# S5 output matrices on two engines, the Toeplitz expansion moved behind the context's steps, and modulation matrices stored by load, in a hybrid S5/RWKV-7 layer

## The chip, the core and the metric

The kernel runs on one core of a Trainium2 chip. The metric is the device time of one execution in microseconds; the time before is the median of three runs. TensorE (PE) multiplies matrices and has a granted clock of one of two levels, 1.2 and 2.4 GHz; the profile gives it as a share of the higher one. VectorE (DVE, V in the code), ScalarE (ACT, A_) and GpSimd (POOL, Pg) compute element by element. SyncE (SP) issues every DMA of this kernel, in order, and waits at the head of its queue for what the next DMA needs.

## The reference

The layer runs over 512 latent tokens x and 256 context tokens of width 1024, with one set of weights:

```python
x = half_ffn(x, mod_x, 0, ...)             # norm, modulate, SwiGLU of 2816, gated add
ctx = half_ffn(ctx, mod_c, 0, ...)
hc = modulate(ctx, norm_g[l, 1], mod_c[3], mod_c[4])
hx = modulate(x, norm_g[l, 1], mod_x[3], mod_x[4])
out_c, ctx_states = token_mixers(hc, 1, zero_states(ctx.shape[0]), p, need_ctx)
out_x, _ = token_mixers(hx, rows, ctx_states, p, True)
x = x + mod_x[5] * out_x
x = half_ffn(x, mod_x, 2, ...)
```

`mod_x` and `mod_c` are nine vectors of 1024, silu(c) @ w_mod + b_mod, so `w_mod` is a matrix of 1024 x 9216. `token_mixers` multiplies by `w_in` and runs two mixers: a bidirectional S5 scan (32 groups of 16 channels, 64 complex states) and a bidirectional RWKV-7 scan. The context gives only its final states. The S5 scan is linear:

```python
hr, hi = _cmul(ab_re, ab_im, h0_re, h0_im)
_, _, s_re, s_im = lax.associative_scan(_s5_combine, (a_re, a_im, xr, xi), axis=0)
y = jnp.einsum('lbgp,gip->blgi', s_re, c_re) - jnp.einsum('lbgp,gip->blgi', s_im, c_im)
```

## The kernel before, in words

Every large product runs on TensorE with the weights split in two parts: `w_loads` issues a DMA of 512 KB into a tile `raw`, `w_split` makes `wh` on ScalarE and `wl` = raw - wh on VectorE or GpSimd, and `mm3` does three matmuls for each block (wh by hi, wh by lo, wl by hi). The list of all weight items in their order is `self.items`; `dense` goes through it.

The order of instructions is fixed when the program is built. All work is written as generators ("streams"); each yields what it needs next: tiles, names of events (`sch.post` posts them), or pairs such as ("V", 600), which mean that the engine's queue may be at most 600 ns ahead of TensorE's. `Plan` keeps an estimate of the time at which each engine is free (`RATE`, `LAT`), treats GpSimd and VectorE's instructions with two SBUF inputs as users of one port (`shared`), costs a DMA by its bytes alone, and always resumes the ready stream with the lowest priority number. `dense` has priority 9, so it fills what the others leave. `w_split` takes VectorE when GpSimd's queue is too far ahead.

S5 runs in blocks of eight tokens. For that `s5_build` (priority S5P = 3) makes, from the powers `pw` of the discretised state matrix, 16 pairs of input matrices (`X`, transposed and stored in DRAM as `GTd`), 16 pairs of output matrices (`H`, stored as `Hd`), and the direct terms of a block (`Kd`). From `Kd` it lays out `KTd` with 15 DMAs of 32 KB and from that the Toeplitz matrices `KTe` with eight of 256 KB. Input matrices are made by GpSimd (six instructions of 128x256 each), output matrices by VectorE in a stream of its own, `outputs`, with two steps ("halves") for each matrix. `GTd` is used by `s5_in` of the context and of x, `Hd` and `KTe` only by `s5_out`, late in the program.

At the start `mods01` and `bg_a` compute modulations 0 to 4: `mod_run` loads tiles `wmod` of 512 KB with four buffers (40 loads) and multiplies each with `zs`; `fill_run` does modulations 5 to 8 later with two buffers (32 loads). The context's FFN and then x's FFN run in `dense`, with the context's `w_in` items mixed into x's FFN.

`ctx_run` holds the context's chain. After the context's norm it adds `s5_build` and the streams of RWKV's preparation (`conv`, `v_rows`, `pn`, `pa`, `pb`), then waits for event `s5b`, for the context's products and for four rounds of `pb` and `v_rows`; then it frees their memory and adds the steps: `rw_solve`, `rw_pre`, `rw_main`, `s5_in`, `s5_rec`. When they are done (events step3 and s5recc) it opens the pools of the next stage and posts `rwc` and `fp0x2`. The last four items of x's FFN (`tail`) wait for `fp0x2`, and the norm that follows waits for `rwc`. After it come x's own `w_in` items, its preparation and its steps (`phase_b2`), the merge and the second FFN (`phase_c`).

Of the kernel before, what the change touches and what calls it, by code (L numbers as in the profile page):

```python
# [11 lines left out]
OP = mybir.AluOpType  # L12
# [3 lines left out]
D, KT = 1024, 8  # L16
# [14 lines left out]
S5V = 600  # L31
S5Q = 3000
MPV = 1200
SPLIT_AT = 0
S5P = 3
# [248 lines left out]
class Kern:  # L284
# [9 lines left out]
    def bank(self, i):  # L294
        return self.psp.tile([128, 512], F32, name=f"b{i}")
# [232 lines left out]
    def mod_run(self, todo, pool, bufs, bank, loaded=None, step=None, done=None):  # L528


        nc, ws = self.nc, []
        steps = [(j, u, k) for j, u in todo for k in (0, 4)]

        def load(n):
            while len(ws) < min(n, len(steps)):
                j, u, k = steps[len(ws)]
                if loaded:
                    loaded(len(ws))
                ws.append(pool.tile([128, 4, 256], F32, name="wmod", bufs=bufs))
                nc.sync.dma_start(ws[-1], self.a["wmod"][j, :, k:k + 4, u * 256:(u + 1) * 256])  # L540
                if loaded and len(ws) == len(steps):
                    loaded(len(ws))

        for n, (j, u, k) in enumerate(steps):
            load(n + bufs)
            if step:
                step(n)
            if k == 0:
                pr = self.bank(bank(j))[:, 0:256]
            yield [ws[n], self.zs]  # L550
            for i in range(4):
                nc.tensor.matmul(pr[i * 32:i * 32 + 32], self.zs[:, k + i], ws[n][:, i], start=k == 0, stop=k == 4)
            if k == 0:
                continue
            row = pool.tile([128, 256], F32, name="mrow")
            nc.scalar.copy(row, pr)
            yield [row]
            pt = self.bank(6)
            for m in range(2):
                nc.tensor.matmul(pt[:, 2 * m:2 * m + 2], row[:, m * 128:(m + 1) * 128], self.sel, start=True, stop=True)  # L560
            ks = slice(2 * u, 2 * u + 2)
            nc.vector.tensor_add(self.mod[:, j, ks], pt[:, 0:4].rearrange("p (m v) -> p m v", v=2),
                                 self.bmod[:, j, ks, None].to_broadcast([128, 2, 2]))
            if done:
                done(j, u)
# [391 lines left out]
    def s5_build(self, sb):  # L957
        nc, a = self.nc, self.a
        V, A_, Pg, PE = nc.vector, nc.scalar, nc.gpsimd, nc.tensor
# [86 lines left out]
        half = lambda n: sb.tile([128, 2, 256], F32, name=n, bufs=1 + (n == "X"))  # L1046
# [6 lines left out]
        todo = [(d, h2) for d in range(2) for h2 in range(8)]  # L1053
# [5 lines left out]
        def load(n, name, src):  # L1059
            t = sb.tile([128, 2, 2, 16], F32, name=name, bufs=2)  # L1060
            d, h2 = todo[n]
            c = slice(d * 16 + h2 * 2, d * 16 + h2 * 2 + 2)
            for i in range(2):
                nc.sync.dma_start(t[:, i], src[i, :, c])
            return t, c

        def outputs():

            nxt = load(0, "hc", a["s5C"])
            for n, (d, h2) in enumerate(todo):  # L1070
                (Ct, c), nxt = nxt, load(n + 1, "hc", a["s5C"]) if n < 15 else None
                yield [Ct, ("V", S5V)]
                H, ms = half("H"), half("mh")
                ks = slice(1, 9) if d == 0 else slice(8, 0, -1)
                for o, (r0, b0, r1, b1, op) in enumerate(terms):
                    V.tensor_mul(r4(ms[:, 0]), bk(pw, r0, ks, c), bb(Ct[:, b0]))
                    V.tensor_mul(r4(ms[:, 1]), bk(pw, r1, ks, c), bb(Ct[:, b1]))
                    if o == 0:
                        V.tensor_tensor(H[:, 0], ms[:, 0], ms[:, 1], op=OP.subtract)
                    else:  # L1080
                        V.scalar_tensor_tensor(H[:, 1], ms[:, 0], -1.0, ms[:, 1], op0=OP.mult, op1=OP.subtract)
                    yield [("V", S5V)]
                for r in range(2):
                    nc.sync.dma_start(self.Hd[2 * h2:2 * h2 + 2, :, d, r].rearrange("e p f -> p e f"),
                                      H[:, r].rearrange("p (e f) -> p e f", e=2))
            self.sch.post("s5h")

        self.sch.add(outputs(), S5P)
        nb, nx = load(0, "hb", a["s5B"]), load(0, "hk", a["s5C"])
        for n, (d, h2) in enumerate(todo):  # L1090
            (B, c), (Ct, c) = nb, nx
# [4 lines left out]
            X, ms = half("X"), half("ms")  # L1096
# [19 lines left out]
            for e in range(2):  # L1116
                o = pk[:, e * 32:(e + 1) * 32]
# [2 lines left out]
            ks = sb.tile([128, 64], F32, name="kst")  # L1120
            A_.copy(ks, pk[:, 0:64])
            nc.sync.dma_start(Kd[d, :, h2 * 64:(h2 + 1) * 64], ks)
        yield ["s5h"]

        Kt, kz = [[half(n).rearrange("p a b -> p (a b)") for n in t] for t in (("X", "H"), ("ms", "mh"))]
        for d in range(2):
# [14 lines left out]
        for s in range(8):  # L1141
            src = [t[s * 16:(s + 1) * 16].rearrange("p (g o) -> p g o", o=16) for t in Kt]
            nc.sync.dma_start(self.KTd[:, :, 14 - s], src[0])
            if s:
                nc.sync.dma_start(self.KTd[:, :, 7 - s], src[1])
        yield [self.KTd]
        for s in range(8):
            nc.sync.dma_start(self.KTe[s], self.KTd[:, :, 7 - s:15 - s].rearrange("i g l o -> i g (l o)"))
        self.sch.post("s5b")


    def win_items(self, r):
# [940 lines left out]
def layout(i):  # L2093
    f = lambda t: np.ascontiguousarray(t)
    o = {}
    o["xin"] = f(i["x"][0].reshape(NX, KT, 128).transpose(2, 1, 0))
    o["cin"] = f(i["ctx"][0].reshape(NCT, KT, 128).transpose(2, 1, 0))
    o["cc"] = f(np.stack([i["c"][0].reshape(KT, 128).T, i["c_ctx"].reshape(KT, 128).T], axis=2))
    o["wmod"] = f(i["w_mod"][0].reshape(KT, 128, 9, 1024).transpose(2, 1, 0, 3))
    o["bmod"] = f(i["b_mod"][0].reshape(9, KT, 128).transpose(2, 0, 1))  # L2100
    o["ng"] = f(i["norm_g"][0].reshape(3, KT, 128).transpose(2, 0, 1))
    o["fg"] = f(i["final_g"].reshape(KT, 128).T)
    g = i["ffn_w_gate"][0].reshape(2, KT, 128, FT, 128).transpose(0, 3, 2, 1, 4)
    u = i["ffn_w_up"][0].reshape(2, KT, 128, FT, 128).transpose(0, 3, 2, 1, 4)
    o["wgu"] = f(np.stack([g, u], axis=2))
    o["wdn"] = f(i["ffn_w_down"][0].reshape(2, FT, 128, 4, 256).transpose(0, 3, 2, 1, 4)).reshape(2, 4, 128, FT, 2, 128)
    gi = np.arange(512).reshape(4, 8, 16).transpose(0, 2, 1).reshape(512)
    win = i["w_in"][0][:, np.concatenate([gi, np.arange(512, 4480)])]
    o["win"] = f(win.reshape(KT, 128, 35, 128).transpose(2, 1, 0, 3))
    o["cw"] = f(i["rwkv_conv"][0].reshape(9, 12, 128).transpose(2, 1, 0))  # L2110
    o["w2"] = f(i["rwkv_w2"][0].reshape(128, 512))
    o["a2"] = f(i["rwkv_a2"][0].reshape(128, 512))
    o["wv"] = f(np.stack([i["rwkv_w0"][0], i["rwkv_a0"][0]]).reshape(2, 2, 4, 128).transpose(3, 0, 1, 2))
    kv = [i["rwkv_k_k"][0], i["rwkv_k_a"][0], i["rwkv_r_k"][0].reshape(512), i["s5_D"][0]]
    o["kv"] = f(np.stack(kv).reshape(4, 4, 128).transpose(2, 0, 1))
    gq = lambda t: np.moveaxis(t.reshape((2, 16, 2) + t.shape[2:]), 2, 0)
    A = lambda t: f(np.moveaxis(gq(t[0]), 3, 1).reshape(128, 32))
    B = lambda t: f(np.moveaxis(gq(t[0]), 3, 1).reshape(128, 32, 16))
    C = lambda t: f(np.moveaxis(gq(t[0]), 4, 1).reshape(128, 32, 16))
    o["s5A"] = np.stack([A(i["s5_A_re"]), A(i["s5_A_im"])])  # L2120
    o["s5B"] = np.stack([B(i["s5_B_re"]), B(i["s5_B_im"])])
    o["s5C"] = np.stack([C(i["s5_C_re"]), C(i["s5_C_im"])])
    o["ldt"] = f(gq(i["s5_log_dt"][0]).reshape(2, 32))
    t4 = lambda w, n: f(w.reshape(4, 128, n, 2, 128).transpose(2, 1, 3, 0, 4)).reshape(n, 128, 8, 128)
    o["wglu"] = t4(i["s5_w_glu"][0][gi][:, gi], 2)
    o["wproj"] = t4(i["s5_w_proj"][0][gi], 4)
    o["wo"] = t4(i["rwkv_w_o"][0], 4)
    o["wout"] = f(i["w_out"][0].reshape(KT, 128, KT, 128).transpose(2, 1, 0, 3))
    o["g2"] = f(i["rwkv_g2"][0])
    o["ln"] = f(np.stack([i["rwkv_ln_g"][0], i["rwkv_ln_b"][0]]).reshape(2, 4, 128).transpose(2, 0, 1))  # L2130
    o["s5D"] = f(i["s5_D"][0].reshape(1, 512))
    return o
# [17 lines left out]
```

## Time and profile before

| what | value |
| --- | --- |
| median of three runs | 1881.02 us (1879.26 to 1885.11) |
| the profiled execution, its own time | 1882.93 us |
| its span, first to last instruction | 1881.2 us |
| TensorE busy | 1681.7 us, 89% |
| VectorE, ScalarE, GpSimd busy | 1008.5, 716.1, 655.1 us |
| mean granted clock of TensorE | 0.935 |
| DMA | 278.42 MB, mean 148 GB/s |

All times below are microseconds from the span's start in this one execution. "Busy" is the union of an engine's instructions; an instruction that is held up while it runs counts as busy. Nearly every row has line L209, that of the helper that records all instructions, so the rows are told apart by the names of their tiles: out<-in.

### The profile page before, as it was taken

Reading aid. Unit: us, or ns where it says so; the run is one execution under the profiler, and the core shown is the slowest. Engines: PE = TensorE matmul, PEld = TensorE weight load, DVE = VectorE, ACT = ScalarE, POOL = GpSimd, SP = SyncE. Lnnn points to the kernel's source line nnn. Section 1 sums busy time; section 2 is a strip of 40 time slices with the busy share of each in tenths; the row PEclk is TensorE's granted clock in tenths of the full one; section 3 lists DMA queues with packets and bytes.
Section 4 is the critical chain, followed back from the end, with each engine's and each line's share of the span. In section 5 each row is a group of like instructions: output and inputs, shape, how many; then the busy total and the mean of one; then the engine's idle time right before and its main releaser. Section 6 shows DMA issues by size and latency. Waiting matters only on the chain. (4 is left out here: it accounts for less than half of the span.)

```text
span 1881.2 us, 33153 instructions
## 1 busy us (share of the span) xinstructions
PE 1681.7 (89%) x13208; PEld 1409.2 (75%) x13208; DVE 1008.5 (54%) x1763; ACT 716.1 (38%) x1200; POOL 655.1 (35%) x799
## 2 busy tenths in 40 slices
PE   6899999899999989768976879969799999999996
PEld 3699997778887877666544657758689988888886
DVE  3376563755558737444788755644357533333335
ACT  3355442445453213434434323434443342222221
POOL 0134231466664313721334526950015321111111
PEclk9999989899999999887988969979899999999998
DMA  9956551335555464424753484637555223233331
GB/s 308 326 179 193 185 157 58 108 104 148 147 162 150 142 195 154 119 94 130 228 182 101 135 252 150 171 108 199 168 200 181 68 79 101 90 99 102 96 96 56
DMA packets 235626, 278.42 MB, mean 148 GB/s; under 512 B 93617, under 2 KB 186801, under 8 KB 234449
## 3 DMA queue, kind: packets, MB, share of 16 engines
q1 hardware_dynamic: 235472, 276.32, 48.3%
q8 instruction: 104, 1.70, 0.4%
q14 instruction: 50, 0.40, 0.1%
HBM read 234.31 MB, written 43.22 MB: 148 GB/s over the span
## 5 line engine op out<-in xcount | busy, mean ns | idle before, releaser
L209 PE MATMUL b<-hx,wh 128*128 128x512 f32 (+1 forms) x2432 | 704.6, 377 | 19.0 <-ACT wh L209 10.6
L209 POOL TENSOR_TENSOR wl<-raw,wh 128x1024 fp32r<-128x1024 f32 x119 | 292.2, 2457 | 805.7 <-ACT wh L209 748.4
L209 PEld LDWEIGHTS b<-hx,wh 128*128 128x128 f32 x2432 | 444.4, 197 | 103.7 <-issue 16.2
L209 PE MATMUL b<-hx,wl 128*128 128x512 f32 (+1 forms) x1216 | 451.4, 371 | 7.5 <-POOL wl L209 6.5
L209 DVE TENSOR_TENSOR wl<-raw,wh 128x1024 fp32r<-128x1024 f32 x154 | 213.2, 1385 | 291.0 <-ACT wh L209 288.7
L209 ACT CAST wh<-raw 128x1024 fp32r<-128x1024 f32 x273 | 283.1, 1046 | 192.8 <-DMA raw<-in_wgu 67.8
L209 PEld LDWEIGHTS b<-hx,wl 128*128 128x128 f32 x1216 | 238.2, 196 | 48.1 <-POOL wl L209 8.8
L209 PE MATMUL b<-ah,wh 128*128 128x512 f32 (+1 forms) x560 | 196.3, 351 | 0.0
L209 PE MATMUL b<-ah,wl 128*128 128x512 f32 (+1 forms) x560 | 194.4, 347 | 0.3 <-POOL wl L209 0.3
L209 PE MATMUL b<-al,wh 128*128 128x512 f32 (+1 forms) x560 | 194.6, 347 | 0.0
L209 PE MATMUL b<-hc,wh 128*128 128x256 f32 x928 | 174.1, 289 | 1.5 <-ACT hc L209 1.2
L209 PEld LDWEIGHTS b<-hc,wh 128*128 128x128 f32 x928 | 146.5, 193 | 12.6 <-issue 10.0
L209 PE MATMUL b<-hc,wl 128*128 128x256 f32 x464 | 132.0, 284 | 0.0
L209 PEld LDWEIGHTS b<-ah,wl 128*128 128x128 f32 x560 | 107.4, 192 | 13.5 <-POOL wl L209 0.5
L209 PEld LDWEIGHTS b<-ah,wh 128*128 128x128 f32 x560 | 107.3, 192 | 12.7 <-issue 0.2
L209 ACT CAST ah<-prod 128x512 fp32r<-128x512 f32 (+1 forms) x68 | 36.6, 538 | 210.6 <-DVE prod L209 210.6
L209 PEld LDWEIGHTS b<-al,wh 128*128 128x128 f32 x560 | 107.3, 192 | 12.5 <-DVE al L209 0.4
L209 ACT ACTIVATE sil<-b 128x512 f32<-128x512 f32 (+1 forms) x68 | 35.0, 515 | 153.6 <-PE b L209 153.5
L209 DVE TENSOR_TENSOR prod<-sil,b 128x512 f32<-128x512 f32 (+1 forms) x68 | 39.6, 582 | 95.2 <-PE b L209 75.7
L209 PEld LDWEIGHTS b<-hc,wl 128*128 128x128 f32 x464 | 89.6, 193 | 0.0
L209 DVE SCALAR_TENSOR_TENSOR x1c<-b,gp,x1c 128x512 f32<-128x512 f32 (+1 forms) x67 | 43.9, 662 | 74.5 <-PE b L209 74.5
L209 PE MATMUL b<-wmod,zs 128*32 128x256 f32 x576 | 55.7, 478 | 23.4 <-DMA wmod<-in_wmod 23.1
(289 smaller groups left out, 2327.4 us busy)
## 6 DMA issues: line engine op xcount, KB each, us to landing
raw<-in_wgu SPq DMA_DIRECT2D x132, 512.0 KB, 3.8
wmod<-in_wmod SPq DMA_DIRECT2D x72, 512.0 KB, 5.5
raw<-in_wdn SPq DMA_DIRECT2D x66, 512.0 KB, 3.7
raw<-in_win SPq DMA_DIRECT2D x49, 512.0 KB, 3.9
gt<-GTd SPq DMA_DIRECT2D x32, 256.0 KB, 4.0
abk<-st SPq DMA_DIRECT2D x8, 1024.0 KB, 5.8
AB<-abk SPq DMA_DIRECT2D x8, 1024.0 KB, 6.9
GTd<-gst SPq DMA_DIRECT2D x16, 256.0 KB, 2.4
```

What stands on the lines that cost most here:

```text
L209: r = f(out, *args, **kw)
```

## The change

Three edits. The array `wmod` is laid out on the host so that the 4 KB that a load brings to a partition are contiguous in DRAM; before they were four runs of 1 KB. The stream `outputs` exists twice: on VectorE from the first matrix on, and on GpSimd from the last one back, entered by `s5_build` itself when all input matrices are done; both take from one list, `left`. GpSimd's writes into the tiles of the input matrices (`hb`, `X`, `ms`). The scalar form of the second half is replaced by a sign flip of the small tile `Ct` and a plain subtraction. And the eight DMAs from `KTd` to `KTe` wait for event `rwc`, with `s5b` posted before them.

```diff
-                nc.sync.dma_start(ws[-1], self.a["wmod"][j, :, k:k + 4, u * 256:(u + 1) * 256])
+                nc.sync.dma_start(ws[-1], self.a["wmod"][j, u, k // 4])
...
-        def outputs():
-
-            nxt = load(0, "hc", a["s5C"])
-            for n, (d, h2) in enumerate(todo):
-                (Ct, c), nxt = nxt, load(n + 1, "hc", a["s5C"]) if n < 15 else None
-                yield [Ct, ("V", S5V)]
-                H, ms = half("H"), half("mh")
+        left = list(range(16))
+
+        def outputs(V, e, names, end):
+
+            nxt = None
+            while left or nxt:
+                nxt = nxt or [left.pop(end)]
+                if len(nxt) == 1:
+                    nxt += load(nxt[0], names[0], a["s5C"])
+                n, Ct, c = nxt
+                d, h2 = todo[n]
+                nxt = None
+                if left:
+                    n = left.pop(end)
+                    nxt = [n, *load(n, names[0], a["s5C"])]
+                yield [Ct, (e, S5V if e == "V" else S5Q)]
+                H, ms = half(names[1]), half(names[2])
                 ks = slice(1, 9) if d == 0 else slice(8, 0, -1)
                 for o, (r0, b0, r1, b1, op) in enumerate(terms):
+                    if o:
+                        V.tensor_scalar(Ct[:, 1], Ct[:, 1], -1.0, None, op0=OP.mult)
                     V.tensor_mul(r4(ms[:, 0]), bk(pw, r0, ks, c), bb(Ct[:, b0]))
                     V.tensor_mul(r4(ms[:, 1]), bk(pw, r1, ks, c), bb(Ct[:, b1]))
-                    if o == 0:
-                        V.tensor_tensor(H[:, 0], ms[:, 0], ms[:, 1], op=OP.subtract)
-                    else:
-                        V.scalar_tensor_tensor(H[:, 1], ms[:, 0], -1.0, ms[:, 1], op0=OP.mult, op1=OP.subtract)
-                    yield [("V", S5V)]
+                    V.tensor_sub(H[:, o], ms[:, 0], ms[:, 1])
+                    yield [(e, S5V if e == "V" else S5Q)]
...
-            self.sch.post("s5h")
+            self.sch.post("s5h" + e)
...
-        self.sch.add(outputs(), S5P)
+        self.sch.add(outputs(V, "V", ("hc", "H", "mh"), 0), S5P)
...
-        yield ["s5h"]
+        yield from outputs(Pg, "P", ("hb", "X", "ms"), -1)
+        yield ["s5hV"]
...
-        yield [self.KTd]
+        self.sch.post("s5b")
+        yield ["rwc", self.KTd]
         for s in range(8):
             nc.sync.dma_start(self.KTe[s], self.KTd[:, :, 7 - s:15 - s].rearrange("i g l o -> i g (l o)"))
-        self.sch.post("s5b")
...
-    o["wmod"] = f(i["w_mod"][0].reshape(KT, 128, 9, 1024).transpose(2, 1, 0, 3))
+    o["wmod"] = f(i["w_mod"][0].reshape(2, 4, 128, 9, 4, 256).transpose(3, 4, 0, 2, 1, 5))
```

S5V is 600 and S5Q is 3000.

## Rows read from the trace of the kernel before

**Rows 1.** The page's first part: busy time, share of the span, instructions.

```profile
PE 1681.7 (89%) x13208; PEld 1409.2 (75%) x13208; DVE 1008.5 (54%) x1763; ACT 716.1 (38%) x1200; POOL 655.1 (35%) x799
```

**Rows 2.** Busy time by stretches: stretch, length, engines, TensorE's clock, DMA share, GB/s.

```profile
core 0: us, PE busy (x) PEld busy (x) DVE busy (x) ACT busy (x) POOL busy (x), PEclk, DMA share, GB/s
0.00:50.00 50.00, 34.88 (x218) 19.30 (x222) 16.94 (x58) 15.94 (x34) 3.68 (x10) 1.00 0.94 310
50.00:100.00 50.00, 41.77 (x389) 30.68 (x381) 19.61 (x40) 17.53 (x34) 8.15 (x9) 0.97 0.95 314
150.00:200.00 50.00, 50.00 (x426) 49.96 (x425) 29.51 (x42) 23.98 (x35) 18.59 (x9) 1.00 0.62 198
...
17.00:21.00 4.00, 2.57 (x18) 0.73 (x18) 2.89 (x10) 2.58 (x7) 0.00 (x0) 1.00 1.10 348
75.00:79.00 4.00, 3.99 (x40) 2.95 (x39) 1.52 (x4) 1.13 (x3) 0.00 (x0) 1.00 1.04 398
```

**Rows 3.** TensorE's waits, 0 to 112 us: total, times, longest.

```profile
PE b L209 <- DMA wmod<-in_wmod: 14.2, 14, 5.0
```

**Rows 4.** Busy time by stretches around the context's chain, columns as in rows 2.

```profile
545.00:663.00 118.00, 115.99 (x654) 94.38 (x653) 86.67 (x145) 45.64 (x71) 47.85 (x34) 1.00 0.52 147
663.00:698.00 35.00, 34.13 (x150) 27.56 (x148) 12.16 (x14) 7.47 (x9) 8.57 (x13) 1.00 0.67 176
698.00:704.00 6.00, 0.61 (x10) 0.40 (x9) 0.00 (x0) 0.00 (x0) 0.00 (x0) 0.78 1.11 331
704.00:751.50 47.50, 45.96 (x394) 36.05 (x391) 36.17 (x66) 14.75 (x42) 15.73 (x15) 0.92 0.52 165
751.50:806.00 54.50, 37.95 (x802) 33.43 (x801) 20.73 (x43) 26.84 (x50) 38.88 (x119) 0.85 0.42 103
```

**Rows 5.** TensorE's timeline from 750 us: start, us, what, idle time before it.

```profile
750.92 0.39 PE L209 MATMUL b<-al,wh 128*128 128x512 f32 x1
751.15 0.39 PE L209 MATMUL b<-ah,wl 128*128 128x512 f32 x1
751.47 1.11 PE L209 MATMUL b<-AB 64*128 64x64 f32 x16
758.39 2.30 PE L209 MATMUL b<-AB 64*128 64x64 f32 x16 [5.82 <-DVE M L209]
```

**Rows 6.** SP's timeline from 662 us: start, us, DMA, count.

```profile
684.73 0.62 SPq L209 DMA_DIRECT2D KTd<-H  x1
...
686.45 6.35 SPq L209 DMA_DIRECT2D KTe<-KTd  x8
692.90 0.64 SPq L209 DMA_DIRECT2D AB<-abk  x1
...
695.98 0.78 SPq L209 DMA_DIRECT2D AT<-lf  x1
...
698.34 0.43 SPq L209 DMA_DIRECT2D gt<-GTd  x1
```

**Rows 7.** Tiles hc and H: ns min/median/max, first and last start, shapes.

```profile
L209 DVE TENSOR_TENSOR mh<-pw,hc x64: 400/419/2627, 349.5 to 661.8; 128x256 f32<-128x256 f32 x64
L209 DVE SCALAR_TENSOR_TENSOR H<-mh x13: 424/425/2508, 567.1 to 662.2; 128x256 f32<-128x256 f32 x13
L209 DVE TENSOR_TENSOR H<-mh x12: 424/426/1809, 582.8 to 661.0; 128x256 f32<-128x256 f32 x12
```

**Rows 8.** Tile st of the context's pb on GpSimd, columns as in rows 7.

```profile
L209 POOL TENSOR_TENSOR st<-kt,em x8: 677/686/1688, 416.8 to 590.0; 64x256 f32<-64x256 f32 x8
```

**Rows 9.** TensorE's waits, 900 to 1000 us.

```profile
PE b L209 <- DMA wmod<-in_wmod: 7.6, 6, 3.2
```

**Rows 10.** Tiles hb and X on GpSimd, columns as in rows 7.

```profile
L209 POOL TENSOR_TENSOR ms<-pz,hb x64: 636/650/1636, 349.2 to 542.6; 128x256 f32<-128x256 f32 x64
L209 POOL TENSOR_TENSOR X<-ms x32: 722/739/1599, 350.8 to 543.3; 128x256 f32<-128x256 f32 x32
```

**Rows 11.** Timeline of GpSimd and VectorE around 600 us.

```profile
599.90 2.57 POOL L209 TENSOR_TENSOR wl<-raw,wh 128x1024 fp32r<-128x1024 f32 x1 [9.15 <-ACT wh L209]
600.25 2.50 DVE L209 SCALAR_TENSOR_TENSOR H<-mh 128x256 f32<-128x256 f32 x1
```

**Rows 12.** GpSimd's timeline from 685 us.

```profile
687.44 0.91 POOL L209 TENSOR_SCALAR_AFFINE_SELECT mask<-ones 64x64 f32<-64x64 f32 x4 [10.18 <-DMA KTd<-H]
```

**Rows 13.** SP's timeline from 804 us.

```profile
806.61 3.69 SPq L209 DMA_DIRECT2D raw<-in_win  x2
830.58 7.57 SPq L209 DMA_DIRECT2D x1d<-x  x16
```

## The prediction

> **What bounds the kernel now.** I read the engine summary first. TensorE is busy 89% of the span and no other engine comes near [rows 1], so an edit counts only where TensorE waits, runs at its lower clock, or is kept waiting by a chain of other work. The busy time by stretches then says where that is, and two of those places touch the change.
>
> The first is the start. In the first two stretches of 50 us the DMA engines are busy 94 and 95% of the time, while TensorE is busy 34.9 and 41.8 us of 50, so it idles 23.4 us in all [rows 2]. The list of waits names the modulation matrices as the largest cause, 14.2 us in 14 waits [rows 3]. From 150 to 200 us TensorE has no gap [rows 2], so time won before that moves everything after it forward.
>
> The second is the end of the context's work. TensorE is full from 545 to 698 us, loses almost all of 698 to 704, is full again to 751.5, and then is busy 38.0 us of 54.5 at a mean granted clock of 0.85 [rows 4]. In the timeline of TensorE the last FFN matmul ends at about 751.5 and only the context's small matmuls follow, up to 806 [rows 5]: the tail of the FFN waits for the context's steps (event fp0x2), and TensorE has nothing else. Going back along the context: its loads (AB, Z, AT, U, gt) stand in SP's queue behind the eight KTe copies, which end at 692.8 [rows 6], and these stand behind the assembly that waits for VectorE's last output at 662.7 [rows 7]. The context's convolutions and its pb stage were done by 592: GpSimd's last st instruction starts at 590.0 [rows 8]. So from 592 to 692 the context waits for S5's output matrices and what follows them, and for nothing else.
>
> **The change part by part.**
>
> *Modulation matrices by load.* Each of the 72 loads keeps its 512 KB but moves runs of 4 KB where it moved runs of 1 KB. Where such loads alone are in flight (17 to 21 us) the DMA engines move 348 GB/s at full share; where nearly all that moves is weights and x in runs of 4 KB (75 to 79 us), 398 GB/s [rows 2]. The 40 loads of the start are 21.0 MB: 60.3 us at the one rate, 52.7 at the other, 7.6 us less, or 0.19 per load. The first 16 loads come before any other work: 3.0 us. The other 24 are worth 4.6 us, and overlap matmuls that fill TensorE for most of that time; I take half, 2.3. The sum is -5 us, bounded by -2 (SP's wait for a free buffer and the latency of a load stay) and -8. The 32 later loads fill gaps between other work; the waits on them from 900 to 1000 us are 7.6 us in 6 waits [rows 9]. 32 times 0.19 is 6 us of transfer, but those gaps follow VectorE's chain, so I take -1, bounds 0 and -3. The Trainium skill, "DMA: Bandwidth & Descriptors", section Specifications, puts the smallest transfer that reaches line rate at 512 bytes, by which 1 KB runs would gain nothing from the new layout; the two rates of this trace disagree. By that rule the sum below would lose both of these terms.
>
> *Output matrices by two engines.* One output is four multiplications and two subtractions. On VectorE they take a median of 0.42 us each, 2.5 us in all [rows 7]; the sign flip of a 32-column tile that replaces the scalar form adds under 0.2. On GpSimd the input matrices have the same six instructions: 4 x 0.65 + 2 x 0.74 = 4.1 us [rows 10]. Of VectorE's 32 halves 25 start after 566 us [rows 7], so 12.5 outputs are still to come when GpSimd finishes its inputs at about 545. Before, VectorE took 96 us for these, 7.7 each, since it also serves the FFN. GpSimd is busy 47.9 us of the 118 between 545 and 663 [rows 4], 41%; in the rest it could make an output every 4.1 / 0.59 = 6.9 us. Both together: 12.5 / (1/7.7 + 1/6.9) = 45 us, so the last output at 590 in place of 662.7. That is the early bound. The late bound is the two engines in each other's way. At 600.25 VectorE's subtraction takes 2.50 us while GpSimd's 2.57 us split runs beside it, six times its median [rows 11]. If the pair is always taken, an output on GpSimd costs 1.6 us more than on VectorE; six of them give 10 us more, and the last output falls at 673.
>
> GpSimd's outputs are also put ahead of what pb has for it: a stream of outputs may run up to 3000 ns ahead (S5Q) while pb asks for under 1000. Six outputs at 4.1 us delay the last pb from 592 to some 617, which alone would not hold the context.
>
> *KTe behind the steps.* The eight copies occupy SP for 6.35 us ahead of the context's loads [rows 6]. Without them the loads start at 686.5; GpSimd's mask, which waits for the last KTd copy until 687.4 [rows 12], limits this to about 5.5 us. At the new place, behind event rwc, the loads of the next weights queue behind them. When rwc falls after the FFN they cost nothing: SP issues only two loads from 806 to 830 [rows 13]. When it falls before, each weight load may be up to 6.35 us late; the loads run about two items of 24 matmuls ahead, so I take +1, bounds 0 and +3.
>
> *What an earlier start is worth.* Call t the time at which the context's loads start, 692.9 before [rows 6]. From there to 806 the chain takes 113 us. TensorE's own work from 692.9 to 806 is 5.1 + 0.6 + 46.0 + 38.0 = 89.7 us [rows 4], so with no gap it would end at 782.6, 23 us earlier; the stretches with clocks of 0.92 and 0.85 could give 3 more. The chain stays covered without any stretching if t is 669 or less. With FFN matmuls between its pieces it stretches: a step has about ten pieces, each may stand behind three matmuls that start 0.23 us apart [rows 5], four steps, so up to 28 us. For t I have 590 + 24 = 614 by the early bound (the 24 us from the last output to the start of KTe) and 697 by the late one. The row at 600 us is real but GpSimd idles more than half of that stretch, so I take the middle, 650. Then the chain ends at 650 + 113 + 28 = 791 with all of the stretching, after the 782.6 of TensorE's own work: 15 us less than 806. Bounds are -26 (no gap, full clock) and 0 (t = 693). Behind 806 the same streams follow in the same order, so I carry the gain to the end undiminished.
>
> **The sum.** -5 - 1 - 15 + 1 = -20 us. The profiled execution took 1882.9 us around its span of 1881.2, so it becomes 1863; it stood 1.9 us above the median of 1881.0, so for the median I say 1861. The best bounds together (-8 - 3 - 26) give 1844; the worst that still have an earlier t (-2 + 3 - 6) give 1876.
>
> **The rivals.** *Two engines in each other's way* (0.20): the last output comes between 663 and 673, t between 686.5 and 697, and only the KTe copies' place counts: -6 to +2 there, with -5 for the start 1870 to 1878, say 1874. For it speaks the row at 600 us, against it GpSimd's idle 59%. The Trainium skill, "SBUF — State Buffer", section "Who interferes with whom", says that a VectorE instruction with two SBUF inputs and a GpSimd instruction that reads SBUF exclude each other for the whole instruction; that is this rival, and the 2.50 us beside 2.57 agree.
>
> *Run length does not matter* (0.12): the start and the later loads give nothing, 1881 - 15 + 1 = 1867. The rate of 398 GB/s is 4 us of trace, in which less was in flight from SP; that is what speaks for it. It is what the Trainium skill, "DMA: Bandwidth & Descriptors", Specifications, would have.
>
> *Everything is recovered* (0.08): t near 614, nothing stretches, 1846.
>
> *Nothing reaches the end* (0.07): the order is fixed at build by a planner, and a changed order further on gives back what was won; 1876 to 1886, say 1880.
>
> *Slower* (0.08): pb starves behind GpSimd's outputs, since they may always be 3000 ns ahead and it needs less than 1000. Its place is the 50 us in which four pb rounds now run (543 to 592). If they start only when all outputs are done, at 655, and take the same 50 us, t is 705 or more. TensorE has run out of FFN work at 751.5, so each us of t beyond 693 is one us of time. It decides from t = 698, where it eats the 5 us of the start; at t = 710, with +1 for KTe, -1 for the fill and -5, the time is 1881 + 17 - 5 = 1893.
>
> **How the numbers follow.** The forecast has 0.45. A measurement of this kernel can tell about 0.3%, 5.6 us, from no change: 1875.4 to 1886.6 counts as the same. Faster holds the forecast, the run length, everything recovered and half of the first rival: 0.45 + 0.12 + 0.08 + 0.10 = 0.75. The same: 0.10 + 0.07 = 0.17. Slower: 0.08. The range 1845 to 1878 leaves out the last two rivals, 0.15. The forecast's own range is 1851 to 1868.
>
> **What would show it.** In the changed profile: modulation loads landing sooner and TensorE's waits on them in the first 112 us near 10 us; the first FFN matmul on x's half of the work some 5 us earlier; H written by GpSimd after 545 and the last output near 610 to 640; AB loaded near 650 with no KTe before it; no gap of 5 us in front of the U,gt matmuls; the small matmuls of the steps mixed with FFN matmuls; and the FFN's tail starting near 785. It is wrong if GpSimd's and VectorE's output instructions take three times their medians, if pb's last instruction comes after 660, if the KTe copies stand in front of a weight load that TensorE waits for, or if the time won by 806 is lost again behind it.

## The result

| kernel | median of its runs | range |
| --- | --- | --- |
| before, beside the changed kernel | 1883.07 us | 1879.26 to 1892.01 (4) |
| changed | 1867.15 us | 1860.21 to 1867.45 (4) |

The ratio is 0.990 with a 95% interval of 0.9857 to 0.9943: about 16 to 19 us faster. Forecast were 1861 us, a range of 1845 to 1878, and "faster" with 0.75. The profiled execution took 1867.45 us around a span of 1865.7. The size was right, in part by luck (below), and the time was won where the forecast put it. But the forecast gave most of it to the second engine; the late KTe copies, to which it allowed 5.5 us, win as much alone, and the two don't add.

**The profile after.** The engine summary of the changed kernel answers to [rows 1]; GpSimd gained 44 us of work, VectorE lost 17:

```profile
PE 1676.7 (90%) x13208; PEld 1403.2 (75%) x13208; DVE 991.2 (53%) x1715; ACT 717.1 (38%) x1200; POOL 699.2 (37%) x863
```

Busy time by stretches of the changed kernel, columns as in [rows 2]; the first four lines answer to [rows 2], the next four to [rows 4], the last two are two whole stages (below):

```profile
0.00:50.00 50.00, 34.79 (x234) 18.86 (x234) 16.96 (x58) 16.30 (x35) 3.68 (x10) 1.00 0.87 316
50.00:100.00 50.00, 44.49 (x419) 34.45 (x418) 22.74 (x48) 19.42 (x36) 8.16 (x9) 1.00 0.91 328
17.00:21.00 4.00, 2.41 (x19) 0.75 (x11) 3.12 (x9) 2.34 (x6) 0.00 (x0) 1.00 0.98 367
71.00:75.00 4.00, 4.00 (x41) 3.03 (x40) 1.52 (x4) 1.58 (x4) 0.00 (x0) 1.00 1.03 412
545.00:663.00 118.00, 114.61 (x647) 94.04 (x646) 70.19 (x93) 40.79 (x62) 78.05 (x94) 1.00 0.57 152
663.00:698.00 35.00, 30.68 (x235) 23.77 (x233) 22.09 (x42) 9.26 (x25) 10.40 (x12) 0.87 0.67 195
698.00:751.50 53.50, 51.11 (x556) 40.67 (x557) 28.36 (x52) 21.22 (x44) 34.66 (x78) 1.00 0.60 167
751.50:806.00 54.50, 49.19 (x696) 43.85 (x694) 27.45 (x54) 25.05 (x48) 24.79 (x59) 0.99 0.37 103
547.20:809.90 262.70, 247.22 (x2135) 204.21 (x2134) 148.82 (x241) 96.41 (x175) 146.05 (x240) 0.97 0.54 149
1088.10:1376.90 288.80, 245.93 (x3333) 205.40 (x3332) 142.44 (x273) 116.63 (x211) 110.92 (x269) 0.89 0.54 159
```

The reader sees two gains. From 50 to 100 us TensorE is busy 44.5 us, where it was 41.8. From 751.5 to 806, where TensorE had run out of FFN work, it is busy 49.2 us at a clock of 0.99, where it was 38.0 at 0.85 [rows 4]. TensorE's waits from 0 to 112 us answer to [rows 3]:

```profile
PE b L209 <- DMA wmod<-in_wmod: 10.3, 11, 5.3
```

**Where the 15.5 us of the span went.** Four DMAs mark the stages: the last store of `Kd`, the first of `x1d` (the context is done), x's first load of AB, and x's load of the gates. The tile view of the stores, with the first and last start of each, gives for the kernel before

```profile
L209 SPq DMA_DIRECT2D Kd<-kst x16: 326/327/333, 365.4 to 552.5; - x16
L209 SPq DMA_DIRECT2D x1d<-x x16: 327/414/425, 830.6 to 837.7; - x16
```

and for the changed one

```profile
L209 SPq DMA_DIRECT2D Kd<-kst x16: 326/327/333, 360.4 to 547.2; - x16
L209 SPq DMA_DIRECT2D x1d<-x x16: 319/414/426, 809.9 to 817.7; - x16
```

| stage | before, us | after, us | difference |
| --- | --- | --- | --- |
| start to last Kd store | 552.5 | 547.2 | -5.3 |
| Kd to x1d (the context's stage) | 278.1 | 262.7 | -15.4 |
| x1d to x's AB load | 281.1 | 278.2 | -2.9 |
| x's AB load to the gates' load | 281.5 | 288.8 | +7.3 |
| from there to the end | 488.0 | 488.8 | +0.8 |

The first two rows are the forecast's -5 and -15. The fourth was not forecast: it gave back nearly a third of what had been won. The same two stages of the kernel before:

```profile
552.50:830.60 278.10, 250.54 (x2135) 209.00 (x2134) 164.25 (x289) 95.56 (x175) 111.10 (x178) 0.95 0.50 140
1111.70:1393.20 281.50, 242.63 (x3344) 202.65 (x3343) 142.06 (x273) 117.33 (x214) 110.57 (x269) 0.92 0.55 163
```

In the context's stage TensorE idled 27.6 us before and 15.5 after, and the clock rose from 0.95 to 0.97. In the later stage it idled 38.9 and then 42.9 us, and the clock fell from 0.92 to 0.89.

**How the context came to its end.** SP's timeline of the changed kernel answers to [rows 6 and 13]:

```profile
661.97 0.36 SPq L209 DMA_DIRECT2D abk<-st  x1
664.42 0.36 SPq L209 DMA_DIRECT2D lf<-a  x1
666.29 0.60 SPq L209 DMA_DIRECT2D AB<-abk  x1
...
766.66 0.45 SPq L209 DMA_DIRECT2D raw<-in_wdn  x1
767.16 6.72 SPq L209 DMA_DIRECT2D KTe<-KTd  x8
778.04 0.40 SPq L209 DMA_DIRECT2D raw<-in_wdn  x1
```

AB is loaded at 666, not 693, and the last thing ahead of it is a store of pb's. The tile view of GpSimd's and VectorE's instructions on output matrices answers to [rows 7]:

```profile
L209 POOL TENSOR_TENSOR ms<-pw,hb x40: 637/648/1716, 552.5 to 620.4; 128x256 f32<-128x256 f32 x40
L209 DVE TENSOR_TENSOR H<-mh x12: 425/752/2516, 346.0 to 627.1; 128x256 f32<-128x256 f32 x12
```

GpSimd's last pb instruction in its timeline answers to [rows 8]:

```profile
660.88 0.74 POOL L209 TENSOR_TENSOR st<-kt,em 64x256 f32<-64x256 f32 x1
```

GpSimd made ten of the sixteen output matrices (40 multiplications), VectorE six. The last output came at 627.1 where it had been 662.2, but pb's last instruction came at 660.9 where it had been 590.0 [rows 8]. The context now waits for pb, not for outputs.

### The profile page after: what moved, and what is told of

It is laid out like the page before. It is cut to its first block, busy times and chain, and to the rows that moved or that the text cites. A ratio compares the mean times of both kernels' runs of the same rounds, so it can differ in the third digit from the quotient of the medians.

```text
span 1865.7 us, 33143 instructions
## 1 busy us (share of the span) xinstructions
PE 1676.7 (90%) x13208; PEld 1403.2 (75%) x13208; DVE 991.2 (53%) x1715; ACT 717.1 (38%) x1200; POOL 699.2 (37%) x863
## 5 line engine op out<-in xcount | busy, mean ns | idle before, releaser
L209 POOL TENSOR_TENSOR wl<-raw,wh 128x1024 fp32r<-128x1024 f32 x113 | 276.4, 2447 | 769.4 <-ACT wh L209 704.9
L209 DVE TENSOR_TENSOR wl<-raw,wh 128x1024 fp32r<-128x1024 f32 x160 | 220.8, 1381 | 285.8 <-ACT wh L209 283.2
L209 ACT CAST wh<-raw 128x1024 fp32r<-128x1024 f32 x273 | 283.0, 1046 | 187.8 <-PE b L209 58.6
L209 PEld LDWEIGHTS b<-ah,wl 128*128 128x128 f32 x560 | 109.0, 195 | 15.4 <-POOL wl L209 2.1
```

The source lines that it names most:

```text
L209: r = f(out, *args, **kw)
```

## The experiments

AB is the start of the context's first load of AB; "solved" is the store of `Tl` by which `rw_solve` ends; the stage is Kd to x1d. All three are of one profiled execution each; ratios are to the kernel before on the same chip.

| kernel | ratio, 95% interval | AB | solved | stage, us |
| --- | --- | --- | --- | --- |
| before | 1 | 692.9 | 755.2 | 278.1 |
| changed | 0.990 [0.9857, 0.9943] | 666.3 | 719.2 | 262.7 |
| changed, again | 0.9886 [0.9854, 0.9919] | 665.6 | 720.0 | 266.2 |
| layout alone | 0.9972 [0.9944, 1.0000] | 688.3 | 750.7 | 283.0 |
| late KTe alone | 0.9931 [0.9905, 0.9958] | 686.3 | 738.4 | 265.6 |
| two engines alone | 0.9918 [0.9891, 0.9944] | 672.3 | 727.1 | 262.3 |
| changed, VectorE alone | 0.9864 [0.9829, 0.9898] | 681.9 | 730.0 | 266.0 |
| the same, again | 0.9900 [0.9872, 0.9927] | 683.8 | 732.9 | 267.7 |
| changed, KTe back | 0.9881 [0.9851, 0.9911] | 670.0 | 725.6 | 262.7 |
| changed, GpSimd not ahead | 0.9916 [0.9883, 0.9950] | 673.1 | 734.7 | 270.9 |
| 4 outputs, stores at the start | 1.0027 [1.0008, 1.0046] | 633.3 | 693.6 | 268.2 |
| 4 outputs, stores late | 0.9922 [0.9892, 0.9953] | 598.7 | 649.9 | 269.2 |
| KTe on ScalarE's queue | 1.0036 [1.0009, 1.0062] | 690.8 | 763.6 | 284.5 |
| before, s5b ahead of KTe | 0.9964 [0.9939, 0.9988] | 688.6 | 746.8 | 271.3 |

**Layout alone.** The kernel before with the two `wmod` lines of the change.

```diff
-                nc.sync.dma_start(ws[-1], self.a["wmod"][j, :, k:k + 4, u * 256:(u + 1) * 256])
+                nc.sync.dma_start(ws[-1], self.a["wmod"][j, u, k // 4])
...
-    o["wmod"] = f(i["w_mod"][0].reshape(KT, 128, 9, 1024).transpose(2, 1, 0, 3))
+    o["wmod"] = f(i["w_mod"][0].reshape(2, 4, 128, 9, 4, 256).transpose(3, 4, 0, 2, 1, 5))
```

> The kernel before with the modulation matrices laid out by load and nothing else; the order of the instructions on every engine stays as it was. Theory: the start is bound by DMA, so TensorE reaches the full stretch behind 112 us about 4 us earlier, and this stays: ratio 0.997 to 0.998, TensorE's waits on the modulation tiles up to 112 us near 10 us (14.2 before). Rival: runs of 1 KB are as fast as runs of 4 KB, or the gain is lost behind the start: 0.999 to 1.001.

Its median was 1881.23 beside 1886.25 us: -5.0, with an interval that just touches no change. Where the loads alone are in flight the busy time by stretches of this kernel shows the changed kernel's rate again, 367 GB/s where [rows 2] has 348:

```profile
17.00:21.00 4.00, 2.41 (x19) 0.67 (x11) 3.17 (x10) 2.34 (x6) 0.00 (x0) 1.00 0.95 367
```

The term of -5 stands, and the clearest sign of it is the last Kd store in all the profiles of this document. It comes at 543.8 to 548.0 us in the eight kernels and repeats with the new layout (4 outputs with stores at the start, below, left out) and at 549.2 to 553.9 in the five with the old one; the means lie 5.1 us apart. By the rule of the Trainium skill, "DMA: Bandwidth & Descriptors", section Specifications (512 bytes already reach line rate), it would have been nothing; these 5.1 us disagree with it, and so do the rates of 348 and 367 GB/s in the same stretch.

**Late KTe alone.** The kernel before with the copies behind `rwc`.

```diff
-        yield [self.KTd]
+        self.sch.post("s5b")
+        yield ["rwc", self.KTd]
         for s in range(8):
             nc.sync.dma_start(self.KTe[s], ...)
-        self.sch.post("s5b")
```

> The kernel before with the eight KTe copies behind event rwc and nothing else. Theory: the context's loads start some 5.5 us earlier (AB near 687 in place of 692.9), the gap of 5.4 us before the U,gt matmuls goes, and the stretch up to the start of the tail becomes 5 to 7 us shorter: ratio 0.996 to 0.998. Rival: the copies were hidden behind what the loads waited for anyway, or they hold up weight loads at their new place: 0.999 to 1.002.

It took 1874.06 us, 12 to 13 less than before, though AB came only 6.6 us earlier. The 5.5 us of the forecast were SP's time. The gap before the U,gt matmuls, which was to go, did not: it was 5.39 us before, and TensorE's timeline of this kernel has

```profile
696.06 1.07 PE L209 MATMUL b<-U,gt 128*64 128x32 f32 x16 [7.96 <-DMA U<-udc]
```

So the gain is not from that gap. What the place was worth shows one step on. In the kernel before, VectorE's timeline has the solve's first operation behind a split of an FFN weight, which had waited 19.9 us:

```profile
706.76 1.23 DVE L209 TENSOR_TENSOR wl<-raw,wh 128x1024 fp32r<-128x1024 f32 x1 [19.94 <-ACT wh L209]
...
709.88 0.18 DVE L209 TENSOR_TENSOR prod<-Tl,AT 128x31 f32<-128x31 f32 x1
```

ScalarE's half of that split waited for the load itself, and SP's timeline of before has that load behind the copies and the context's loads of [rows 6]:

```profile
685.45 0.56 SPq L209 DMA_DIRECT2D raw<-in_wgu  x1
...
699.57 0.33 SPq L209 DMA_DIRECT2D raw<-in_wgu  x1
```

With the copies gone from there, VectorE's timeline begins the solve 15 us sooner, and what it waits for is the context's own load:

```profile
694.94 0.19 DVE L209 TENSOR_TENSOR prod<-Tl,AT 128x31 f32<-128x31 f32 x1 [9.62 <-DMA U<-udc]
```

So the copies cost the 6.4 us of SP, and beyond that they made an FFN weight late, which stood ahead of the solve in VectorE's order. The planner's order differs between the two kernels, so two traces don't part these; the last experiment does so in part.

**Two engines alone.** The kernel before with the two streams of outputs; layout and KTe as before. Shown is the place where GpSimd's stream is entered; the streams themselves are as in the change.

```diff
-        yield ["s5h"]
+        yield from outputs(Pg, "P", ("hb", "X", "ms"), -1)
+        yield ["s5hV"]
```

> The kernel before with the output matrices on two engines and nothing else. AB near 673 to 677 (692.9 before). New theory, that any start of the context's steps before some 686 is enough: 0.992 to 0.994 of before, like the KTe copies' move alone (0.9931), and not the sum of the two in the changed kernel. Rival, that the copies in front of the context's loads are what cost: 0.998 to 1.001, with the gap before the U,gt matmuls still there.

**Changed, VectorE alone.** The changed kernel without GpSimd's share, run in two batches.

```diff
-        yield from outputs(Pg, "P", ("hb", "X", "ms"), -1)
```

> The changed kernel with all output matrices made by VectorE; layout and KTe as changed. Theory: the second engine is worth the larger part, AB is loaded near 682 in place of 666, and the time lies 5 to 10 us above that of the changed kernel, near 0.994 to 0.996 of before. Rival (two engines in each other's way, so that the second one brings nothing): within 3 us of the changed kernel, 0.990 to 0.993.

> The changed kernel with all output matrices by VectorE, timed beside the changed kernel on the same chip. New theory: with AB loaded at 682 the FFN already covers the context's steps, so the second engine's 16 us of earlier start bring nothing and the two kernels are within 3 us. First theory: the changed kernel is 5 to 10 us faster.

**Changed, KTe back.** The changed kernel with the copies at their old place.

```diff
-        self.sch.post("s5b")
-        yield ["rwc", self.KTd]
+        yield [self.KTd]
         for s in range(8):
             nc.sync.dma_start(self.KTe[s], ...)
+        self.sch.post("s5b")
```

> The changed kernel with the KTe copies back in front of the context's loads; two engines and layout as changed. AB near 672. New theory: t is early enough with or without the copies, so the time is that of the changed kernel within 3 us, and the copies' place and the second engine can stand in for each other. Rival: the copies cost by standing right before the context's loads wherever that is, in SP's queue and in traffic; then 5 to 10 us above the changed kernel, and the gap before the U,gt matmuls is back.

**The changed kernel again**, beside the last two.

> The changed kernel unaltered, beside the others of this batch. 0.989 to 0.992 of before, as when it was first timed. Its stretch from x's stored residual to the gates' loads, 7 us longer than before in the first profile with 61 us at the lower clock there, comes back within 3 us of before's if that was the clock of one execution, and stays longer if it is in the order of the instructions.

These five read together. Each of the two edits alone takes the stage from 278 to between 262 and 266 us. Both together leave it there: taking the second engine away (0.9864, 0.9900) or the late KTe away (0.9881) changes nothing that can be told from the changed kernel (0.9900, 0.9886). Two profiles of the changed kernel differ by 3.5 us in this stage, and layout alone by 4.9 from the kernel before, whose order it has; so differences of 5 us in that column mean nothing by themselves. The two edits substitute for each other. The traces show one reason: in the changed kernel with KTe back, SP's timeline has the copies from 654.4 to 662.2, and AB follows at 670.0, behind pb's last store at 667.7. The second engine has put the copies into a wait for pb, where they hold up nothing of the context. VectorE still waits 10.73 us there for a split of an FFN weight right ahead of the solve (at 684.36), as in the kernel before, but the solve is early enough to bear it. The changed kernel with VectorE alone is as fast as the changed kernel.

**How much earlier would help.** First, the changed kernel with only 4 of 16 output matrices computed; the other 12 are left out, and constants are stored in their place at the start of the stream.

```diff
-        left = list(range(16))
+        left = list(range(4))
...
+        for d, h2 in todo[4:]:
+            for r in range(2):
+                nc.sync.dma_start(self.Hd[2 * h2:2 * h2 + 2, :, d, r].rearrange("e p f -> p e f"),
+                                  self.ones[:, None, :].to_broadcast([128, 2, 128]))
```

> The changed kernel with 4 of the 16 output matrices computed; for the other 12 a constant tile is stored, so their arithmetic is left out. pb and not the outputs then holds the context, AB near 625. New theory: beyond t = 686 nothing is to be had, so the time is that of the changed kernel within 4 us, up to what 12 outputs less free on VectorE. First theory, one us for one us down to t = 669 and less below: 5 or more faster. Rival: one us for one us throughout, 30 or more faster.

This came out slower, 1890.43 us, but not by what it was meant to test: it was already 20 us late at the last Kd store (567.4), ahead of the stage in question. Its stage was 268.2 us. Then the same stores behind `rwc`, ahead of the copies, with `yield [("S", 600)]` behind each matrix's pair:

> The changed kernel with 4 of the 16 output matrices computed; the constant tiles for the other 12, whose arithmetic is left out, are stored behind event rwc, where they hold up nothing that the context waits for (in the first such kernel they held up SP and TensorE near 350 us). AB near 615. New theory: the stretch from the last Kd store to x's stored residual stays at 262 to 268 us, as in the changed kernel, and the time within 5 us of the changed kernel's 0.989. Rival: it shrinks by 10 us or more.

AB came at 598.7, 68 us before the changed kernel's, and the stage took 269.2 us all the same, though SP's timeline has `rwc` and the stores by 697.4 us. Stores and copies hold SP for 21 us there, but TensorE's waits from 690 us to the end of the stage, 3.8 us, are none of them for a load. Its stretch in the busy time shows TensorE with 18.3 us of idle time, where late KTe alone, with AB at 686, has 19.6:

```profile
544.70:813.90 269.20, 250.90 (x2137) 205.00 (x2136) 124.48 (x225) 95.32 (x175) 96.17 (x171) 0.97 0.51 144
```

So from about 686 us down an earlier start of the context's steps is worth nothing here: 599, 633, 666 and 686 give stages of 269, 268, 263 to 266, and 266 us. But 686 us is no threshold by itself. With the copies on ScalarE's queue (below) AB comes 136.9 us after the last Kd store, with late KTe 137.1, and the stages are 284.5 and 265.6 us. What the stage follows is the end of the solve, the column "solved", counted from the last Kd store: up to 189 us the stage is 262 to 271 us, and at 196, 203, 205 and 210 us it is 271, 278, 283 and 284.5. The idle time that remains with an early solve, 14 to 20 us, does not depend on the start.

**GpSimd not ahead.** The changed kernel with GpSimd's outputs at most 500 ns ahead, in place of 3000.

```diff
-                yield [Ct, (e, S5V if e == "V" else S5Q)]
+                yield [Ct, (e, S5V if e == "V" else 500)]
...
-                    yield [(e, S5V if e == "V" else S5Q)]
+                    yield [(e, S5V if e == "V" else 500)]
```

> The changed kernel with GpSimd's outputs at most 500 ns ahead in place of 3000, so that pb, which asks for under 1000, gets GpSimd first. Theory: pb's last load to DRAM (662.0 in the changed kernel) comes near 610, then the last output holds the context, near 635 to 645, and AB is loaded near 660; since FFN matmuls already cover most of the context's steps, only 0 to 4 us come of it: 0.988 to 0.991 of before. Rival: the start of the context's steps is still worth one us for one us: AB 10 or more earlier and the time lower by as much. If neither moves, what holds the context is not pb.

The last store of pb's `st` came at 621.7 in place of 662.0, so pb did get GpSimd first. But the stores of the outputs then ended at 652.3 in place of 627.9, and AB came at 673.1, later by 7 us and not earlier. Outputs and pb are one budget of GpSimd's time, and what one gains the other loses. The ratio can't be told from that of the changed kernel.

**KTe on ScalarE's queue.** The kernel before with the eight copies issued by ScalarE, to take them out of SP's way without moving them in time.

```diff
-            nc.sync.dma_start(self.KTe[s], ...)
+            nc.scalar.dma_start(self.KTe[s], ...)
```

> The kernel before with the eight KTe copies at their old place in the order, but issued by ScalarE's queue, so that SP's queue is free and the traffic stays; the order on TensorE, VectorE and GpSimd is unchanged. If SP's queue was the cost of the copies: AB loaded near 687, the gap before U,gt 2 us or less, and the time 5 us or more lower. If their traffic was: AB issued near 687 but landing late, the gap of 5 us stays, ratio 0.999 to 1.001.

The ratio is 1.0036, slower if anything. AB now comes 2.6 us after the last KTd store (688.25 to 690.85), before 8.2 [rows 6]. But ScalarE's timeline shows that this engine computes nothing for 21.65 us:

```profile
689.96 1.72 ACTq L209 DMA_DIRECT2D KTe<-KTd  x2
700.60 5.08 ACTq L209 DMA_DIRECT2D KTe<-KTd  x6
705.71 0.62 ACT L209 CAST ah<-prod 128x512 fp32r<-128x512 f32 x1 [21.65 <-DMA KTe<-KTd]
```

VectorE's matching operation waited 17.7 us for it and TensorE 7.7. The issuing itself takes 6.80 us in two runs, about what it takes on SyncE; between the second copy and the third ScalarE's queue stands still for 8.9 us. The pause ends when the second of SP's two loads of Z lands (issued at 692.2, 8.4 us to landing); whether the copy waited for that load was not tried. So this kernel adds a wait of its own, and does not price SP's queue. It shows that what stands behind the copies is late on this queue too, and it points to their traffic: AB takes 8.0 us from issue to landing here, 6.6 in the kernel before and 5.9 with late KTe.

**Which of the things behind the copies counts.** The kernel before with `s5b` posted ahead of the copies, and nothing else.

```diff
+        self.sch.post("s5b")
         yield [self.KTd]
         for s in range(8):
             nc.sync.dma_start(self.KTe[s], ...)
-        self.sch.post("s5b")
```

> The kernel before with event s5b posted ahead of the eight KTe copies instead of behind them, and nothing else. The context's loads (AB, Z, AT, U, gt) then stand ahead of the copies in SP's queue, as they do with the copies at their late place, but the second of the two FFN weight loads that follow still stands behind the copies. Theory one, the copies cost because FFN weights stand behind them: the second weight load is issued near 700 us as before, ScalarE and VectorE wait for it as before, TensorE's gap near 700 us stays at 4 to 6 us though the context's loads come 6 us sooner, and the time is within 0.3% of before. Theory two, they cost because the context's loads stand behind them: AB near 686 us, the solve's first VectorE operation near 695 us (before 709.9), x1d's store near 815 us (before 830.6), no gap of 5 us, and a ratio near that of the late copies, 0.993. If both count, the solve's first operation comes between 697 and 707 us and the ratio lies between 0.994 and 0.998.

SP's timeline of this kernel shows that it parts the two: the context's loads ahead of the copies, one FFN weight still behind them.

```profile
688.56 0.60 SPq L209 DMA_DIRECT2D AB<-abk  x1
...
694.39 0.34 SPq L209 DMA_DIRECT2D raw<-in_wgu  x1
695.12 7.45 SPq L209 DMA_DIRECT2D KTe<-KTd  x8
702.67 0.63 SPq L209 DMA_DIRECT2D raw<-in_wgu  x1
```

The solve begins early, but stops in the middle, as VectorE's timeline shows:

```profile
697.23 0.19 DVE L209 TENSOR_TENSOR prod<-Tl,AT 128x31 f32<-128x31 f32 x1 [9.63 <-DMA U<-udc]
...
701.89 2.42 DVE L209 TENSOR_TENSOR Tl<-Tl,prod 128x192 f32<-128x192 f32 x1
709.63 1.23 DVE L209 TENSOR_TENSOR wl<-raw,wh 128x1024 fp32r<-128x1024 f32 x1 [5.31 <-ACT wh L209]
```

The ratio is 0.9964, in the band in which both count. The gap before the U,gt matmuls is 7.96 us here too, where the second theory had it gone. From the AB load to the end of the solve are 58.2 us here (688.6 to 746.8), 52.1 with late KTe (686.3 to 738.4): the weight behind the copies is worth 6 us inside the solve. The stage is 271.3 us, 6.8 below before and 5.7 above late KTe. By these, one execution each, and by the two ratios (0.9964 and 0.9931, whose intervals overlap), something like half of what the copies' place cost was the context's loads and half the FFN weight; the shares are not shown more closely than that. What the copies' traffic adds is within the first half, and no experiment parts it from SP's time.

## Why the prediction was right, and where it was not

**Right.** The layout: forecast -5 at the start, measured -5.3 at the last Kd store and -5.0 in the median of layout alone; TensorE's waits 10.3 us where "near 10" was written. The later loads: -1 forecast for the fill is within the scatter. The context's stage: -15 forecast, -15.4 measured. KTe at its new place: at 767 us it took 6.72 us of SP, and TensorE waits for none of the weight loads that stood behind it; +1 forecast, nothing found. The first matmul of the FFN's tail comes at 785.1 us (805.9 before), where "near 785" was written. t was put at 650 and came at 666.

**The sum was right by two errors that cancelled.** The forecast's t of 650 leaves out the 5 us of the start; the measured 666.3 has them, so it is 671.6 on that scale, 21.6 later. The stretching, 28 us in the forecast, was 5.9 (143.6 us from AB to x1d, 137.7 before). 671.6 + 113 + 5.9 = 790.5, where the forecast had 791: that the -15 came out is luck, though the mechanism did take place. The steps behind it failed as follows. The first is "Both together: 12.5 / (1/7.7 + 1/6.9) = 45 us". GpSimd's rate was right: its 20 halves run from 552.5 to 621.9, 6.9 us an output. VectorE's was not. The costliest groups from 545 to 663 us of the kernel before have, for the splits of FFN weights,

```profile
L209 POOL TENSOR_TENSOR wl<-raw,wh 128x1024 fp32r<-128x1024 f32 x13 | 32.6, 2511 | 52.0 <-ACT wh L209 46.5 <-DMA hc<-in_s5C 5.6
...
L209 DVE TENSOR_TENSOR wl<-raw,wh 128x1024 fp32r<-128x1024 f32 x8 | 10.1, 1262 | 11.8 <-ACT wh L209 11.8
```

and of the changed kernel

```profile
L209 POOL TENSOR_TENSOR wl<-raw,wh 128x1024 fp32r<-128x1024 f32 x4 | 9.7, 2422 | 10.6 <-ACT wh L209 6.6 <-DMA hc<-in_s5C 4.0
L209 DVE TENSOR_TENSOR wl<-raw,wh 128x1024 fp32r<-128x1024 f32 x16 | 21.5, 1342 | 26.1 <-ACT wh L209 26.0
L209 DVE TENSOR_TENSOR H<-mh 128x256 f32<-128x256 f32 x5 | 4.4, 877 | 2.4 <-DMA Hd<-H 2.3
```

Nine splits left GpSimd, and VectorE took eight more: `w_split` turns to VectorE when GpSimd's queue is ahead. VectorE finished only 2.5 outputs in this stretch (five H). The splits are a part of the cause and not all of it: they took 11.4 us more of VectorE's busy time and 14.3 us more of waiting, while its busy time in the stretch fell from 86.7 to 70.2 us. With GpSimd at most 500 ns ahead VectorE had nearly as many splits, 14, and made 5.5 outputs in the same stretch:

```profile
L209 DVE TENSOR_TENSOR H<-mh 128x256 f32<-128x256 f32 x11 | 7.4, 674 | 4.2 <-DMA Hd<-H 3.9
```

How far GpSimd's outputs run ahead in the plan, which has the two engines' instructions take turns on one port, is therefore a likely part of the cause; the shares were not tried. The last output came at 627, not 590. The forecast's own guess of 650 for t allowed for a mishap of that size, of another cause.

The second is pb. "Six outputs at 4.1 us delay the last pb from 592 to some 617" became ten outputs and 662. This is the slower rival's mechanism, and it did take place. It cost nothing, since t came to 666 and not to 698, where that rival's point of decision lay.

**"About 5.5 us" for KTe's place is the step whose size was wrong.** By itself it brought 12 to 13 us (late KTe alone) and 12.5 in the stage. The 12.5 is read from one execution each, in a stage that scatters by 5 us; the 12 to 13 are medians. The forecast counted what the copies take of SP and looked only at the context's loads behind them; the FFN weight that stands behind those, and in VectorE's order ahead of the solve's work, was not followed.

**"The chain stays covered ... if t is 669 or less"** failed as well: t = 686 with late KTe has the same stage as t = 666, and t = 599 gains no more. That is why the large edit (a second engine, AB 27 us earlier) adds nothing to the small one. The stretching was real in kind, but grows with the head start: the chain from AB to x1d takes 144 us after, 138 before, and 215 with AB at 599.

**"I carry the gain to the end undiminished"** failed. The later stage lost 7.3 us. It did so again in the second profile of the changed kernel (287.0 us, clock 0.90):

```profile
1096.00:1383.00 287.00, 244.63 (x3336) 204.34 (x3336) 142.68 (x273) 117.11 (x214) 110.73 (x269) 0.90 0.54 160
```

The loss sits with x's first solve: from x's AB load to the store that ends it are 50.8 us before (1111.7 to 1162.5) and 58.4 after (1088.1 to 1146.5). The longer solve goes with the second engine: the four profiles in which GpSimd makes outputs up to 3000 ns ahead have 56.8 to 59.8 us for it, the seven in which VectorE makes all of them 50.1 to 52.7. The stage itself is parted less well: 283.7 to 288.8 against 280.1 to 284.3, with means some 4 us apart, so the 7.3 us of the one pair is more than the order explains. Of the other three profiles, GpSimd not ahead has 51.6 us and a stage of 285.7, the two with 4 outputs 52.7 and 50.8 with stages of 290.5 and 281.0. Which change of order brings the longer solve, and what lengthens the stage without it, was not tried and stays open. What the rival "nothing reaches the end" named, an order that gives back further on, is thus part of the result.

**Two engines in each other's way.** GpSimd's multiplications keep their median of 648 ns where the input matrices had 650 [rows 10]; VectorE's H has a median of 752 ns and a maximum of 2516, where it was 426 [rows 7]. The pair costs some, and did not decide.

## What to carry to other kernels

When a block of DMAs is moved out of a queue, follow every entry that stood behind it, and then every engine whose next instruction waits for one of those: the price is the lateness at the end of that walk, not the queue time. Before a chain is made earlier by a second engine, ask how early is early enough; here an edit of two lines, or a second engine, reached that point alone, and both together moved the start another 16 to 18 us forward for nothing. Work that is put on an idle engine pushes what a planner would have put there onto the engine that was to be relieved.

## What the runs showed of the hardware

The eight copies from DRAM to DRAM, 256 KB each, hold the queue that issues them: 6.35 to 7.45 us in all in the rows shown on SyncE, and 6.80 us on ScalarE, which computes nothing meanwhile nor in the pause of 8.9 us between its copies. And more idle time of TensorE came with a lower clock and more busy time: in the changed kernel's stage from 1088 to 1377 us 4.0 us more of idle time, a mean clock of 0.89 in place of 0.92 and 3.3 us more of busy time for no more matmuls (3333 and 3344), 7.3 us in all; in its second profile 3.5 us, 0.90 and 2.0 us (3336). No experiment changed the idle time alone, so which brings the other is not shown.
